# The last four feature tiles of a gated MLP's down projection: plain products or a fourth chunk of block products

## The chip, the cores and the metric

The kernel runs on one core of one Trainium2 chip. The metric is device time of one execution in microseconds (us); the time before is the median of three runs. A profile is one execution taken by the hardware profiler. TensorE is called PE there (PEld is its loading of weights), VectorE DVE, ScalarE ACT, GpSimd POOL; SP's queue issues nearly all the DMAs.

## What is computed

One encoder block on x of shape (1024 positions, 1024 channels), in float32: two parallel convolution modules, then the part that matters here, a gated MLP with 2816 features and a last RMSNorm.

```python
h = rmsnorm(x, norm_ffn_g[l])
g = dwconv(jnp.einsum("bsd,df->bsf", h, w_gate[l]), conv_ffn_w[l])   # 3 taps over positions
v = jnp.einsum("bsd,df->bsf", h, w_up[l])
x = x + jnp.einsum("bsf,fd->bsd", jax.nn.silu(g) * v, w_down[l])
...
return rmsnorm(x, norm_final_g)
```

## The kernel before

Channels lie on the 128 partitions, positions along a row of 1024, split in two halves of 512 (h = 0, 1). The 2816 features are 22 tiles (`f`), the 1024 output channels are 8 blocks (`d`). Every matmul is done with numbers split in a high and a low part: `split` (L130) writes `hi` by a copy on ScalarE and `lo` by a subtraction, in the down stage on VectorE, and a product of 128 x 128 by 128 x 512 is three matmuls.

**Block products.** To save matmuls the kernel treats two feature tiles and two output blocks and the two halves as 2 x 2 blocks and computes seven products where the plain way has eight. On the side of the activations these need seven operands: `B11`, `B21`, `B22` and four differences `T1` to `T4`. For a pair of feature tiles `ff_done` (L607) forms the differences with four subtractions on GpSimd and stores all seven, 256 KB each, in DRAM (`yd`). On the side of the weights `Sums` (L504) forms `S1` to `S4` on GpSimd. `Pair` has one method for each product, `m1` to `m7`, which accumulate in three PSUM banks `a`, `b`, `c` and after each step hand a sum to `Down`'s `after1` to `after7` (L868 on), which add it to the residual block: mostly on VectorE (`add`, L862), after `m1` by a copy on ScalarE and an add on GpSimd (`add_copy`).

**The down stage.** 18 of the 22 tiles go through block products, in three chunks (`NCH`) of three pairs (`PPC`). A chunk is passed over by four objects `Down`, one for each two output blocks, taken as two couples; while one couple multiplies, the weights of the next are loaded and split (`prep1` to `prep3`), and in a chunk's second couple each operand of the next chunk is loaded as soon as its last product is done (`load_op`, L823). The residual blocks `xf` are loaded from `x2d` in DRAM; blocks 3 to 7 (`xd3`, `xr0`, `xr1`) lie where the MLP's temporary tiles `t` lay, and their loads (`load_xd`, L906) are issued when those are released.

**The tail.** The last four tiles (`NTAIL`) go to `ytail` undivided. After the three chunks they are multiplied the plain way: for each half and each output block 4 x 3 matmuls into one bank (`tail_mm`). First all eight blocks of h = 0, then h = 1. `done` (L1026) adds the bank to the residual block on VectorE, squares it on ScalarE, and adds the square to `accs[h]` on VectorE; `scale` (L1022) multiplies the block by the norm's weight on ScalarE. When h = 0 is complete a matmul with ones sums over the channels (`total3`), ScalarE takes the root, VectorE the reciprocal `rf`, and GpSimd scales the eight blocks of h = 0 (`fin`, L1035) beside the products of h = 1. The last block of h = 1 is handled in three pieces (`PIECES`: 192, 192, 128 positions): total, root, reciprocal, scaling of eight blocks (five on VectorE, three on GpSimd) and store.

**What sets the order.** TensorE's order is written out by hand throughout; in the last part, from h = 1 on, those of VectorE, ScalarE and GpSimd too. Before that the other engines' instructions are placed by a scheduler, which puts an instruction where its inputs and buffers allow it. Each engine takes its instructions strictly in order, and SP its DMAs, so that one that waits holds up all behind it.

## Time and profile before

| | us |
|---|---|
| median of 3 runs | 1000.53 (1000.17 to 1000.76) |
| the profiled execution, device time | 1000.93 |
| its span in the trace | 999.1 |
| TensorE busy | 967.5 |
| matmuls of the tail, lines 152 to 154, 192 in all | 25.3 + 24.9 + 24.9 of busy time |
| GpSimd busy | 477.0 |
| DMA | 112.56 MB, 113 GB/s in the mean |

A row of the timeline gives the start in us, the length, the engine, the line, the operation with output and inputs, and in brackets how long the engine had stood idle before and what it waited for. A group row gives busy time and the mean length in ns, then the idle time ahead of it by cause. Matmuls overlap: each shows as 0.39 us, but the next starts 0.23 later.

### The profile page before, as it was taken

Reading aid. Unit: us, or ns where it says so; the run is one execution under the profiler, and the core shown is the slowest. Engines: PE = TensorE matmul, PEld = TensorE weight load, DVE = VectorE, ACT = ScalarE, POOL = GpSimd, SP = SyncE. Lnnn points to the kernel's source line nnn. Section 1 sums busy time; section 2 is a strip of 40 time slices with the busy share of each in tenths; the row PEclk is TensorE's granted clock in tenths of the full one; section 3 lists DMA queues with packets and bytes.
Section 4 is the critical chain, followed back from the end, with each engine's and each line's share of the span. In section 5 each row is a group of like instructions: output and inputs, shape, how many; then the busy total and the mean of one; then the engine's idle time right before and its main releaser. Section 6 shows DMA issues by size and latency. Waiting matters only on the chain.

```text
span 999.1 us, 11602 instructions
## 1 busy us (share of the span) xinstructions
PE 967.5 (97%) x4208; PEld 790.8 (79%) x4208; DVE 755.6 (76%) x888; ACT 452.8 (45%) x632; POOL 477.0 (48%) x303
## 2 busy tenths in 40 slices
PE   7999999999999999999999999999998999999994
PEld 5788888888878887788888888888886787878883
DVE  7899999999578897855655565565569798796556
ACT  7454422234564456434444443444457263544353
POOL 4289754353853006554455456365336744352006
PEclk9999999999999999999999999999999999999998
DMA  6211111113554204143143133134284663643105
GB/s 257 85 44 63 43 45 61 42 64 106 193 190 153 76 0 158 64 148 106 64 145 108 64 124 129 64 101 141 70 287 130 220 207 96 194 127 109 61 1 169
DMA packets 63274, 112.56 MB, mean 113 GB/s; under 512 B 5488, under 2 KB 27120, under 8 KB 62960
## 3 DMA queue, kind: packets, MB, share of 16 engines
q1 hardware_dynamic: 62640, 110.65, 33.1%
q10 hardware_dynamic: 576, 1.17, 0.3%
q8 instruction: 33, 0.54, 0.2%
q14 instruction: 25, 0.20, 0.1%
HBM read 84.79 MB, written 27.00 MB: 112 GB/s over the span
## 4 chain that ended last, share of the span: by engine, by line
PE 81%; DVE 9%; ACT 3%; issue 2%; DMA 1%; POOL 1%; POOLq 0%; SPq 0%; DVEq 0%; ACTq 0%
PE a L557 30%; PE mm L166 20%; PE c L557 15%; PE b L557 7%; DVE r L93 2%; PE c L692 1%; PE a L692 1%; PE mm L153 1%; PE mm L152 1%; PE mm L154 1%; PE y L154 1%; PE y L152 1%; PE y L153 1%; DMA raw<-wgate 1%; ACT whi L131 1%
## 5 line engine op out<-in xcount | busy, mean ns | idle before, releaser
L166 PE MATMUL mm<-r,whi 128*128 128x512 f32 x576 | 155.8, 389 | 0.0
L557 PE MATMUL a<-r,whi 128*128 128x512 f32 x472 | 145.7, 390 | 0.4 <-ACT a L542 0.4
L323 DVE SCALAR_TENSOR_TENSOR cv<-u,cst,cv 128x512 f32<-128x512 f32 x203 | 138.9, 751 | 1.7 <-ACT cv L317 1.2
L511 POOL TENSOR_TENSOR s<-raw,s 128x512 f32<-128x512 f32 (+1 forms) x31 | 57.5, 1854 | 161.5 <-DVE wlo L93 161.5
L166 PEld LDWEIGHTS mm<-r,whi 128*128 128x128 f32 x576 | 108.1, 188 | 22.6
L557 PE MATMUL c<-r,whi 128*128 128x512 f32 x392 | 121.1, 390 | 0.0
L93 POOL TENSOR_TENSOR wlo<-raw,whi 128x1024 fp32r<-128x1024 f32 x30 | 77.5, 2586 | 88.0 <-ACT whi L131 88.0
L131 ACT ACTIVATE whi<-raw 128x1024 fp32r<-128x1024 f32 (+1 forms) x68 | 69.2, 1020 | 103.5 <-PE mm L166 32.0
L557 PEld LDWEIGHTS a<-r,whi 128*128 128x128 f32 x472 | 88.4, 188 | 19.7 <-ACT a L542 0.8
L511 POOL TENSOR_TENSOR s<-up 128x512 f32<-128x512 f32 (+1 forms) x31 | 42.0, 1354 | 116.7 <-DMA up<-wup 96.8
L557 PE MATMUL a<-r,wlo 128*128 128x512 f32 x236 | 92.2, 391 | 2.8 <-DVE wlo L93 2.8
L166 PE MATMUL mm<-r,wlo 128*128 128x512 f32 x288 | 90.0, 389 | 0.0
L557 PEld LDWEIGHTS c<-r,whi 128*128 128x128 f32 x392 | 73.8, 188 | 16.0
L542 ACT ACTIVATE a<-a 128x512 f32<-128x512 f32 x80 | 47.5, 595 | 66.9 <-PE a L557 64.2
L131 ACT ACTIVATE whi<-s 128x1024 fp32r<-128x1024 f32 (+1 forms) x52 | 52.5, 1010 | 53.5 <-PE c L557 39.8
L557 PE MATMUL c<-r,wlo 128*128 128x512 f32 x196 | 76.5, 390 | 0.0
L635 DVE TENSOR_TENSOR t<-a,c 128x512 f32<-128x512 f32 x40 | 27.5, 687 | 64.4 <-ACT a L542 38.1
L557 PE MATMUL a<-r,ahi 128*128 128x512 f32 x224 | 70.5, 396 | 1.4 <-ACT a L542 1.4
L557 PE MATMUL b<-r,whi 128*128 128x512 f32 x232 | 71.4, 389 | 0.0
L93 DVE TENSOR_TENSOR wlo<-s,whi 128x1024 fp32r<-128x1024 f32 (+1 forms) x52 | 64.2, 1236 | 5.8 <-ACT whi L131 5.7
L131 ACT ACTIVATE r<-r 128x512 fp32r<-128x512 f32 x71 | 43.8, 628 | 49.8 <-DMA r<-ydB 23.3
L166 PEld LDWEIGHTS mm<-r,wlo 128*128 128x128 f32 x288 | 54.1, 188 | 11.2
(214 smaller groups left out, 2142.0 us busy)
## 6 DMA issues: line engine op xcount, KB each, us to landing
raw<-wgate SPq DMA_DIRECT2D x22, 512.0 KB, 4.9
up<-wup SPq DMA_DIRECT2D x20, 512.0 KB, 3.6
raw<-win SPq DMA_DIRECT2D x18, 512.0 KB, 3.2
ydT<-t SPq DMA_DIRECT2D x36, 256.0 KB, 3.4
r<-ydT SPq DMA_DIRECT2D x36, 256.0 KB, 3.3
raw<-wout SPq DMA_DIRECT2D x16, 512.0 KB, 3.4
ydB<-t SPq DMA_DIRECT2D x27, 256.0 KB, 5.0
r<-ydB SPq DMA_DIRECT2D x27, 256.0 KB, 4.5
```

Source lines behind the costliest of these rows:

```text
L93: eng.tensor_tensor(out=out, in0=a, in1=b, op=ALU.subtract)
L131: nc.scalar.activation(hi, y, AF.Copy)
L152: nc.tensor.matmul(out, whi, hi, start=first, stop=False)
L153: nc.tensor.matmul(out, whi, lo, start=False, stop=False)
L154: nc.tensor.matmul(out, wlo, hi, start=False, stop=last)
L166: nc.tensor.matmul(outs[h], w, a[h][z], start=s0, stop=s1)
L323: nc.vector.scalar_tensor_tensor(fin if k == KC - 1 else acc, src, w, acc, ALU.mult, ALU.add)
L511: self.eng.tensor_tensor(out=self.t[:, i * self.w : (i + 1) * self.w], in0=a, in1=b, op=op)
L542: nc.scalar.activation(t, b, AF.Copy)
L557: nc.tensor.matmul(out, w[wz][:, k, :], x[xz], start=first and k + wz + xz == 0, stop=k == n - 1 and wz == 1, skip_group_check=not first)
L635: nc.vector.tensor_tensor(out=out, in0=a, in1=b, op=op)
L692: nc.tensor.matmul(out, w[wz][:, k, :], xz, start=first and k == 0 and wz == 0 and xz is hi, stop=not first and k == 3 and wz == 1)
```

## The change

The plain tail is gone. The four last tiles become two more pairs, which `ff_done` treats like the others, and a fourth chunk of two pairs (`NPL`): `fin4`, four objects `Down` (`a4`, `b4`, `c4`, `d4`) with six matmuls for each product. Their order is written out by hand: first the products that complete h = 0 of all eight blocks, `m1`, `m6`, `m2`, `m7`, `m4`, then `m5` and `m3`, which complete h = 1. `final` takes the place of `done`: squares are added on VectorE for h = 0 and for h = 1 on GpSimd (`eng`). The last square of h = 0 is not added but given to `total3` as a second operand. An activation with the root's function (`warm`) is written ahead of the last two products of h = 0. In the first couple, `after5` goes by ScalarE and GpSimd instead of VectorE. In the last scaling VectorE takes all eight blocks of the first two pieces, and GpSimd takes three blocks of the last piece only.

```diff
-NTAIL = NF - 2 * NCH * PPC
+NPL = NF // 2 - NCH * PPC
...
-        if f >= NF - NTAIL:
-            nc.sync.dma_start(ytail[f - (NF - NTAIL)], cc)
-            return
         ys[f] = cc
...
+    def count(ch):
+        return PPC if ch < NCH else NPL
...
+            self.h12, self.h34 = h12, h34 or w34[self.e]
...
         def after5(self):
-            self.add(1, 1, self.c)
+            if self.early:
+                self.add_copy(1, 1, copy_of(self.c, "c5"))
+            else:
+                self.add(1, 1, self.c)
...
+    fin4 = [Down(NCH, dp) for dp in range(2)]
+    fin4 += [Down(NCH, 2 + e, rblocks[28 + 2 * e : 30 + 2 * e], rblocks[32 + 2 * e : 34 + 2 * e]) for e in range(2)]
+    couples.append(fin4[:2])
...
-        for i, pair in enumerate(couples):
+        for i, pair in enumerate(couples[:-1]):
             ch = pair[0].ch
-            reload = i % 2 and ch + 1 < NCH
+            reload = i % 2
...
-    def total3(a):
+    def total3(*a):
         m = bank2("total")
-        nc.tensor.matmul(m, ones, a, start=True, stop=True)
+        for i, x in enumerate(a):
+            nc.tensor.matmul(m, ones, x, start=i == 0, stop=i == len(a) - 1)
         return m
...
-    def done(b, d, h):
+    def final(d, h, eng=nc.vector, first=0, alone=None):
         x = half(xf[d], h)
-        nc.vector.tensor_tensor(out=x, in0=b, in1=x, op=ALU.add)
-        sq = scr("sq") if d else accs[h]
+        sq = scr("sq") if d != first else accs[h]
         nc.scalar.activation(sq, x, AF.Square)
-        if d and (h, d) != (1, KD - 2):
-            nc.vector.tensor_tensor(out=accs[h], in0=accs[h], in1=sq, op=ALU.add)
+        if d not in (first, alone):
+            eng.tensor_tensor(out=accs[h], in0=accs[h], in1=sq, op=ALU.add)
+        scale(d, h)
         return sq
...
+    a4, b4, c4, d4 = fin4
     with tc.manual_schedule(engines={nc.tensor.engine}):
...
+        for p in (c4, d4):
+            p.m7()
+        nc.scalar.activation(warm, eps_r, AF.Sqrt)
+        c4.m4()
+        final(5, 0)
+        d4.m4()
+        s7 = final(7, 0, alone=7)
...
     with tc.manual_schedule(engines={e.engine for e in (nc.tensor, nc.vector, nc.scalar, nc.gpsimd)}):
...
+        a4.m5()
+        b4.m5()
+        m0 = total3(accs[0], s7)
+        std = scr("std")
+        nc.scalar.activation(std, m0, AF.Sqrt, bias=eps_r, scale=1.0 / D)
+        final(1, 1, first=1)
+        final(3, 1, nc.gpsimd, 1)
+        nc.vector.reciprocal(rf[:, :H], std)
+        c4.m5()
+        final(5, 1, nc.gpsimd, 1)
+        d4.m5()
+        final(7, 1, nc.gpsimd, 1)
+        a4.m3()
+        final(0, 1, nc.gpsimd, 1)
+        b4.m3()
+        final(2, 1, nc.gpsimd, 1)
+        for dd in range(KD):
+            fin(dd, 0, 0, H, nc.gpsimd)
+            if dd % 2:
+                store(dd // 2, 0, 0, H)
+        c4.m3()
+        s6 = final(4, 1, first=1, alone=4)
+        d4.mul(d4.c, "S4", "B22", False)
...
-        for (a, b), m in zip(PIECES, ms):
+        for (a, b), m, n in zip(PIECES, ms, (KD, KD, 5)):
...
             for d in range(KD):
-                fin(d, 1, a, b, *((nc.vector, rp) if d < 5 else (nc.gpsimd,)))
+                fin(d, 1, a, b, *((nc.vector, rp) if d < n else (nc.gpsimd,)))
```

What this does to the order of instructions, at three places. First SP's queue at the passage from the MLP into the down stage, before; `ytail` is the store of a finished tile, the lines below load residual blocks 3 to 7:

```order
L616 DMA ytail_1798<-t_5658 128x1024
L616 DMA ytail_1798<-t_5678 128x1024
L907 DMA xd3_5699<-x2d_1790 128x1024
L907 DMA xr0_5700<-x2d_1790 128x1024 x2
L907 DMA xr1_5701<-x2d_1790 128x1024 x2
```

and now, where `t_5668` and `t_5687` are tiles 20 and 21, and `t_5693` and `t_5694` their differences, which GpSimd forms:

```order
L623 DMA ydB11_1791<-t_5668 128x512
L623 DMA ydT1_1795<-t_5693 128x512
L623 DMA ydB21_1793<-t_5687 128x512
L623 DMA ydB22_1797<-t_5687 128x512
L623 DMA ydT2_1792<-t_5693 128x512
L623 DMA ydT3_1794<-t_5694 128x512
L623 DMA ydT4_1796<-t_5694 128x512
L914 DMA xd3_5720<-x2d_1790 128x1024
L914 DMA xr0_5721<-x2d_1790 128x1024 x2
L914 DMA xr1_5722<-x2d_1790 128x1024 x2
```

The loads of x now stand behind seven stores, three of which wait for GpSimd's last subtractions. Second, GpSimd at the same place, now; `s` are sums of weights, `a1` and `c5` copies of PSUM banks that are added to residual blocks:

```order
L90 TENSOR_TENSOR t_5693<-t_5668 128x512
L510 TENSOR_TENSOR s_5799<-up_5796 128x384
L90 TENSOR_TENSOR xd0_5497<-xd0_5497,a1_5861 128x512
L510 TENSOR_TENSOR s_5799<-s_5799,raw_5779 128x384
L90 TENSOR_TENSOR t_5693<-t_5687,t_5693 128x512
L90 TENSOR_TENSOR t_5694<-t_5687,t_5668 128x512
L90 TENSOR_TENSOR t_5694<-t_5687,t_5693 128x512
L90 TENSOR_TENSOR xd0_5497<-xd0_5497,c5_5886 128x512
L510 TENSOR_TENSOR s_5789<-raw_5772,s_5789 128x384
```

Before, the four rows that write `t` and the one that adds `c5` were not there. Third, the end of GpSimd's program: before, the first half's scaling by `rf` followed directly on the last add to a residual block of the three chunks; now five sums of squares (`acc31`) stand ahead of it:

```order
L90 TENSOR_TENSOR xr1_5722<-xr1_5722,a0_7267 128x512
L1002 TENSOR_TENSOR acc31_7089<-acc31_7089,sq_7393 128x512
L1002 TENSOR_TENSOR acc31_7089<-acc31_7089,sq_7406 128x512
L1002 TENSOR_TENSOR acc31_7089<-acc31_7089,sq_7418 128x512
L1002 TENSOR_TENSOR acc31_7089<-acc31_7089,sq_7429 128x512
L1002 TENSOR_TENSOR acc31_7089<-acc31_7089,sq_7440 128x512
L1008 TENSOR_TENSOR xd0_5497<-xd0_5497,rf_7367 128x512 x2
```

Of the early activation with the root's function ScalarE's order shows the following: it stands (L1052) near the start of the program, behind the first two activations of the opening norm's loop (the difference at the end of this section); at the end the load of the table is where it was, directly ahead of the first half's root:

```order
L1000 ACTIVATE sq_7363<-xr1_5722 128x512
L995 ACTIVATE xr1_5722<-xr1_5722,cst_90 128x512
L1063 ACT_TABLE_LOAD
L1063 ACTIVATE std_7389<-total_7386,eps_r_92 128x512
L1000 ACTIVATE acc31_7089<-xd0_5497 128x512
```

and ScalarE's order at the start of the program, as a piece of the difference (`c` is a block of `x`, `acc` and `sq` belong to the first norm):

```order
 L221 ACTIVATE acc_118<-c 128x512
 L224 ACTIVATE sq<-c 128x512
+L1052 ACTIVATE warm<-eps_r 128x1
 L213 ACTIVATE r_94<-c,cst 128x512 x2
 L224 ACTIVATE sq<-c 128x512 x2
```

One row is new there; the load of the table at the end has not moved.

More of the change, by code (lines that the diff above doesn't have):

```diff
@@ new lines, in block_kernel @@
+        for p in (a4, b4):
+            p.m1()
+        for p in couples[-2]:
+            p.m3()
+        load_op(NCH, "B22")
+        for p in (a4, b4):
+            p.prep3()
+        for p in (a4, b4):
+            p.m6()
+        for p in (c4, d4):
+            p.prep1()
+        for p in (a4, b4):
+            p.m2()
+            final(2 * p.dp, 0)
+        for p in (c4, d4):
+            p.prep2()
+            p.prep3()
+        for p in (a4, b4):
+            p.m7()
+        for p in (c4, d4):
+            p.m1()
@@ new lines, in block_kernel @@
+        for p in (a4, b4):
+            p.m4()
+            final(2 * p.dp + 1, 0)
+        for p in (c4, d4):
+            p.m6()
+        for p in (c4, d4):
+            p.m2()
+            final(2 * p.dp, 0)
+        for p in (c4, d4):
+            p.m7()
+        nc.scalar.activation(warm, eps_r, AF.Sqrt)
[3 more added lines that the diff above has]
+        s7 = final(7, 0, alone=7)
+    rf = rup.tile([P, S], F32, tag="up", name="rf")
+    with tc.manual_schedule(engines={e.engine for e in (nc.tensor, nc.vector, nc.scalar, nc.gpsimd)}):
+        a4.m5()
[21 more added lines that the diff above has]
+        d4.mul(d4.c, "S4", "B22", False)
+        last = d4.c
+        x = half(xf[KD - 2], 1)
```

109 lines of the change are left out of this document (26 added, 83 removed).

## The prediction

> **What bounds the kernel now.** I read the page's first block and the windows by stage, then the chain of work that ended last, then the timelines around the places where TensorE stops.
>
> ```profile
> span 999.1 us, 11602 instructions
> ...
> PE 967.5 (97%) x4208; PEld 790.8 (79%) x4208; DVE 755.6 (76%) x888; ACT 452.8 (45%) x632; POOL 477.0 (48%) x303
> ...
> 750.00:800.00 50.00, 45.50 (x189) 36.03 (x189) 42.22 (x43) 24.61 (x38) 35.11 (x22) 0.97 0.57 179
> ...
> 950.00:999.00 49.00, 35.76 (x160) 28.92 (x158) 29.95 (x46) 20.61 (x33) 16.21 (x17) 0.92 0.26 86
> ```
>
> In the window rows the length is followed by the busy times of PE, PEld, DVE, ACT and POOL. TensorE is the limit of the down stage; it loses 4.5 us in 750 to 800 and 13 us at the very end, and little between. So a matmul that is removed is worth its slot only if what stands behind the last matmul gets no longer. The chain says what stands there:
>
> ```profile
> 909.37 4.08 PE c L557 x18
> ...
> 968.91 0.70 DVE xd L1028
> ...
> 986.13 1.28 DVE rp L1092
> 987.43 0.34 ACT rf L1093
> 987.79 1.15 DVE xd L1037 x4
> ```
>
> One matmul is 4.08 / 18 = 0.227 us, and from 968.9 us the chain has left TensorE for adds, squares, reciprocals and the last scaling.
>
> **The matmuls.** The old tail has 16 groups of 4 x 3 matmuls, 192; the fourth chunk has 4 pairs x 7 products x 6, 168. That is 24 x 0.227 = 5.4 us less TensorE time; the second operand in the first half's sum gives back 0.9.
>
> ```profile
> 933.57 0.39 PE L557 MATMUL a<-r,alo 128*128 128x512 f32 x1
> ...
> 965.28 0.86 PE total L1019 x2
> ```
>
> Between chunk three's last A22 product and the last product that the first half needs lie 150 matmuls (chunk three's S4, 18, and 11 steps of 12): 933.8 + 150 x 0.227 = 967.8, in PSUM at **968.0**. Call it T. In the old order the second half's squares begin at 963.3 (below), with seven groups of 12 matmuls, 19 us, still to run; now the first half's statistics start at T, and only 6 products of 6 matmuls (8.2 us) are left to run beside them. This decides the end.
>
> **The end, forward from T.** Durations, from the timeline:
>
> ```profile
> 2.47 0.20 ACT L208 ACTIVATE warm<-eps_r 128x1 f32<-128x1 f32 x1
> ...
> 963.32 0.63 ACT L1030 ACTIVATE acc<-xd 128x512 f32<-128x512 f32 x1 [1.33 <-DVE xd L1028]
> ...
> 963.98 0.72 ACT L1024 ACTIVATE xd<-xd,cst 128x512 f32<-128x512 f32 x1
> ...
> 966.71 0.69 DVE L1032 TENSOR_TENSOR acc<-acc,sq 128x512 f32<-128x512 f32 x1 [0.70 <-ACT sq L1030]
> ...
> 967.45 1.28 ACT L1067 ACT_TABLE_LOAD   x1
> ...
> 968.75 0.69 ACT L1067 ACTIVATE std<-total,eps_r 128x512 f32<-128x512 f32 x1
> ...
> 970.91 3.35 DVE L1069 RECIPROCAL rf<-std 128x512 f32<-128x512 f32 x1
> ...
> 984.43 0.42 ACT L1088 ACTIVATE std<-total,eps_r 128x192 f32<-128x192 f32 x1 [0.25 <-PE total L1085]
> ...
> 992.20 0.95 DVE L1092 RECIPROCAL rp<-std 128x128 f32<-128x128 f32 x1
> ```
>
> Block 5's product is in PSUM at 966.65, added by 967.4 and squared on ScalarE by 968.05; ScalarE scales it, squares block 7 until 969.4, scales it until 970.15, and then loads the root's table until 971.4. The table is not loaded early: the added activation waits for nothing, so the new order has it among ScalarE's first rows, where the same table is already in place (at most 0.20 us, as the first activation of that kind took), and the load ahead of the late root stays. That costs little. VectorE adds block 7 from T on and ends its last sum at 969.5 (2 x 0.69); the two-operand total (2 x 0.86) then ends at 971.2, so the table is late by 0.2 us. The root ends at 972.1, the reciprocal at 975.5. TensorE stands still for 1.5 us at T, which is covered: its last product ends at 979.5, and others end later.
>
> For now ScalarE is the chain: a square and a scale, with gaps 1.38 us, for each block of the second half. Two are done before 975; block 5's add waits behind the reciprocal and ends at 976.1, and then the squares end at 976.7, 978.1, 979.4, 980.8 and 982.2. GpSimd adds five of them, the last from 980.8 on. What such a sum costs there:
>
> ```profile
> L90 POOL TENSOR_TENSOR xd<-xd,a 128x512 f32<-128x512 f32 x10 | 18.9, 1897 | 15.2 <-ACT a L542 15.2
> ...
> L90 POOL TENSOR_TENSOR xr<-xr,a 128x512 f32<-128x512 f32 x6 | 7.7, 1287 | 5.8 <-ACT a L542 5.6 <-DMA xr<-x2d 0.2
> ...
> 977.55 1.66 DVE L1032 TENSOR_TENSOR acc<-acc,sq 128x512 f32<-128x512 f32 x1 [0.70 <-ACT sq L1030]
> ...
> 974.40 5.95 POOL L1037 TENSOR_TENSOR xd<-xd,rf 128x512 f32<-128x512 f32 x4 [63.03 <-DVE rf L1069]
> ...
> 993.54 1.28 POOL L1037 TENSOR_TENSOR xr<-xr,rf 128x128 f32<-128x128 f32 x3 [0.95 <-ACT rf L1093]
> ...
> 995.89 0.90 SPq L1046 DMA_DIRECT2D outT<-xr  x2
> ```
>
> A 128x512 sum on GpSimd takes 1.29 us beside a quiet VectorE and 1.90 beside a busy one, and VectorE's own sum 0.69 or 1.66. I take 1.4: the sum is complete at 982.2. The first piece's total ends 1.2 us later (six passes of 192 columns, 1.0, and the 0.25 before the root), the root at 983.8, the reciprocal at 985.1, the copy at 985.5. Then VectorE scales all eight blocks (8 x 0.29 = 2.3), where it had five: a piece now takes 1.28 + 0.36 + 2.3 = 3.9 us, before 3.0 (from 986.1 to 992.2 for two). Two pieces end at 991.8; the third (0.95, 0.3, five of at most 0.29) by 994.5. GpSimd meanwhile scales the first half, 8 blocks from 982.2, and here I take 1.35, near the quiet row, since VectorE's scaling reads its factor from PSUM: 993.0, then its three short ones (1.28), 994.3. SP's queue holds the first half's last store at 993.0 and six more behind it at 0.45 each, the last issued at 996.2 instead of 996.8. The tail so gains **0.6 us**; with 1.29 throughout 1.0, with 1.49 (5.95 / 4) it loses 0.3, with 1.9 some 4. So 5.4 us of matmuls are nearly all given back.
>
> The Trainium skill's page "SBUF — State Buffer" (section SBUF: two separate sides) says that a VectorE operation with two SBUF inputs and a GpSimd operation that reads SBUF take one port in turns, the loser blocked for a whole instruction. The 0.69 and 1.66 agree. By that rule GpSimd's scaling would run at the quiet 1.29, and the tail gains 1.0.
>
> **The passage into the down stage.** The last four feature tiles now take part in the block products: per pair four GpSimd subtractions, and seven stores of 256 KB for two of 512 KB. All of it stands on SP ahead of loads.
>
> ```profile
> 740.00:750.00 10.00, 10.00 (x45) 8.21 (x44) 4.20 (x6) 3.98 (x9) 2.47 (x2) 1.00 0.91 342
> ...
> 746.40 0.63 ACT L131 ACTIVATE r<-r 128x512 fp32r<-128x512 f32 x1 [6.02 <-DMA r<-ydB]
> ...
> 776.33 3.35 PE L557 MATMUL a<-r,r 128*128 128x512 f32 x7 [2.76 <-DVE r L93]
> ...
> 780.74 2.02 POOL L90 TENSOR_TENSOR xd<-xd,a 128x512 f32<-128x512 f32 x1
> ...
> 781.52 2.32 DVE L614 TENSOR_TENSOR t<-t 128x1024 f32<-128x1024 f32 x1
> ...
> 784.30 0.38 SPq L907 DMA_DIRECT2D xd<-x2d  x1
> ...
> 789.37 0.69 DVE L863 TENSOR_TENSOR xd<-xd,a 128x512 f32<-128x512 f32 x1 [1.91 <-DMA xd<-x2d]
> ...
> 801.30 2.52 DVE L93 TENSOR_TENSOR r<-r 128x512 fp32r<-128x512 f32 x2 [2.29 <-ACT r L131]
> ...
> 804.24 4.24 PE L557 MATMUL a<-r,r 128*128 128x512 f32 x18
> ...
> 834.52 4.35 PE L557 MATMUL a<-r,r 128*128 128x512 f32 x18 [1.41 <-DVE xd L863]
> ```
>
> First pair: before chunk zero's B21 load stand 0.8 MB more; at 342 GB/s (the last column) that is 2.3 us on a load ScalarE already waits 6.0 for. VectorE then works nearly without pause until TensorE's 2.76 us wait at 776; an add moved forward and small pauses take up most of it. **+0.3**, between 0 and 2.3.
>
> Second pair: the product of tile 21 ends at 783.8, and before, the loads of x for blocks 3 to 7 went out at 784.3. Now three subtractions come between (GpSimd is busy until 784.5 with one more ahead, then 3 x 1.5, to 789), and the load of block 3 goes into a buffer that the T2 store must have read (issued at 786, landing about 3.4 later by its row): out at 790, landed, with the 5.1 us of before, at 795 instead of 789.4. VectorE stands at its add of block 3 until then; behind it wait both S4 splits, two adds and the first xr add, which TensorE needs by 804.2: 795 + 6 operations (4.7 us) = 799.7, so 4.5 us remain. The loads of chunk one's B11 go out later too, but VectorE had 2.29 us of waiting there. After that it works without a pause up to the 1.41 us wait at 834.5, which gets some longer: **+0.6**. Ends: -1.4 (two 0.69 us adds leave VectorE for ScalarE and GpSimd, and the wait goes) and +6 (GpSimd at 1.90 per operation, loads landing in 8).
>
> Fourth chunk: its slots from 933.8 on put the first pair's B21 product at 944.7, and only then is a buffer free for the third pair's weights, needed at 948.8. ScalarE (0.63) and VectorE (0.69) split them, each behind one or two splits of sums that GpSimd delivers at about 945; by their rows they are ready at 947.6, 1.2 us early. The sums have 256 columns, which no row shows (192 columns take 0.59 us below, 384 take 1.28); I take 0.8. **+0.3**, between 0 and 2.
>
> ```profile
> ydT<-t SPq DMA_DIRECT2D x36, 256.0 KB, 3.4
> ...
> L511 POOL TENSOR_TENSOR s<-raw,s 128x384 f32<-128x384 f32 x12 | 15.3, 1279 | 47.7 <-DVE wlo L93 47.7
> ...
> L1037 POOL TENSOR_TENSOR xr<-xr,rf 128x192 f32<-128x192 f32 x6 | 3.4, 587 | 3.3 <-ACT rf L1093 3.3
> ```
>
> Sum: -0.6 + 0.3 + 0.6 + 0.3 = +0.6. The profiled execution took 1000.93 us (1.8 around its span), 0.40 over the median of 1000.53, so 1001.5 against the one and **1001.1** against the other.
>
> **Rivals.** (1) *Slower: VectorE behind the x loads.* If block 3 lands after 799.5 the 804.2 product waits, and VectorE, late by as much, makes the wait at 834.5 longer again. GpSimd at 1.90 and a slower store and load give 802.5, 3 us late: 1003.5 to 1006. For it: that queue has two more links than before; against: 4.5 us of room. 25%. (2) *Faster.* The two adds taken off VectorE end the 1.41 us wait, the first pair costs nothing, and the tail gains 1.0: 1000.5 - 2.4, 998.1, less if the 776 wait shrinks. For it: VectorE ends each of these waits; against: GpSimd's new work blocks it. 18%. (3) *Late weights in the fourth chunk* if GpSimd's short sums take 1.3: TensorE waits 3 us, T is 971 and the whole end moves: 1003.5. 7%. (4) *The table costs more than its row.* That the early load doesn't do what it says is in the forecast already; had it worked, it would save 0.2 us. But if a switch held ScalarE for twice the 1.28 of its row, every later square would come 1.3 later: 1002.4. Against it: the root starts 0.02 us after the load. The Trainium skill's page "ScalarE: Activation LUTs" (What ACT_TABLE_LOAD costs) does put a drain of 1380 ns on top of each load; the trace shows none here. 4%. Forecast: 46%.
>
> **How the numbers follow.** This kernel can be told from no change at about 0.2%, 2.0 us: 998.5 to 1002.5. Faster is rival 2 (18%), slower rivals 1 and 3 (32%), the rest the same (50%). The range cuts a tenth at each side: 997.5 from rival 2's better half, 1005.5 from rival 1's worse.
>
> **What would show it.** PE 168 matmuls for 192, and T near 968 plus the waits; the table load still directly ahead of the late root; the last square near T + 14 with VectorE and TensorE waiting; eight GpSimd scalings after it; in 784 to 800 VectorE idle for a DMA 6 us longer. Wrong if GpSimd's sums or x loads are much slower, or VectorE's backlog at 834 vanishes.

## The result, and the profile after

The changed kernel takes **1008.12 us** (median of 4 runs, 1007.47 to 1012.91), the one before on the same chip 1000.35: a ratio of 1.0089 (95% 1.0076 to 1.0101), 7.8 us slower. The forecast, no difference, was wrong, and the time lies outside its range. The profiled execution took 1007.47 us with a span of 1005.3, so 6.2 of the 7.8 us can be followed in the traces; the rest is scatter between executions.

The page's first lines after, and the windows by stage in the columns of before:

```profile
span 1005.3 us, 11721 instructions
PE 965.8 (96%) x4186; PEld 788.1 (78%) x4186; DVE 772.0 (77%) x908; ACT 460.1 (46%) x653; POOL 514.6 (51%) x332
...
800.00:850.00 50.00, 45.20 (x190) 36.28 (x189) 41.82 (x54) 21.80 (x35) 23.28 (x18) 0.97 0.55 173
850.00:900.00 50.00, 50.00 (x221) 41.10 (x220) 41.78 (x54) 24.36 (x39) 25.29 (x19) 1.00 0.58 174
...
950.00:1000.00 50.00, 38.23 (x162) 30.66 (x160) 38.48 (x66) 27.74 (x48) 22.88 (x22) 0.92 0.18 60
```

TensorE is busy 1.7 us less: the 22 matmuls that are gone (24 less, 2 more in the total) are 5.0 us, but others ran longer. From 850 to 950 it doesn't stop. What is new is in 800 to 850: 190 matmuls, where before had 214. TensorE's timeline after shows the two waits there:

```profile
815.05 0.73 PE L556 MATMUL a<-r,ahi 128*128 128x512 f32 x2 [1.78 <-DVE xr L864]
...
839.13 3.27 PE L556 MATMUL a<-r,r 128*128 128x512 f32 x7 [2.98 <-DVE xd L864]
```

The second is the wait that stood at 834.52 with 1.41 us: it ends **4.6 us later**. Behind it come only 7 matmuls in 3.27 us. The windows after, right behind it, say why (the seventh number is the granted clock); the second fence is the same stretch of the run `e14` below, after a wait of 2.97 us:

```profile
839.00:842.00 3.00, 2.87 (x7) 2.32 (x8) 3.00 (x5) 0.47 (x1) 0.25 (x1) 0.50 0.01 3
842.00:845.00 3.00, 3.00 (x15) 2.43 (x14) 1.97 (x4) 0.00 (x0) 0.00 (x0) 0.96 0.00 0
```

```profile
839.00:842.00 3.00, 2.94 (x13) 2.46 (x14) 3.00 (x5) 0.82 (x2) 0.18 (x1) 1.00 0.01 3
```

TensorE ran at half clock for 3 us: it did 7 matmuls where it does 13 at the full clock, so 1.4 us were lost.

To compare kernels I use TensorE's **lag**: how much later than in before's trace the first `b` product of a couple starts.

| couple starts in before at | 765.90 | 800.16 | 828.86 | 859.25 | 887.96 | 917.36 |
|---|---|---|---|---|---|---|
| lag after, us | 0.70 | 0.71 | 3.05 | 6.06 | 6.05 | 5.41 |

So 5.4 us come from the passage into the down stage. The last product that the first half needs is in PSUM at 973.6 (last row 973.20 + 0.40), forecast 968.0: 5.6, so the fourth chunk brought 0.2 more. From there to the end of the span pass 31.7 us, where the forecast amounts to 30.5 (last store issued at 996.2, then the 2.3 of before), so the tail cost 0.6 where it was to gain 0.6. 5.4 + 0.2 + 0.6 = 6.2.

The tail's timeline after, of ScalarE, GpSimd, TensorE and SP:

```profile
975.75 1.28 ACT L1063 ACT_TABLE_LOAD   x1
...
982.47 5.36 POOL L1002 TENSOR_TENSOR acc<-acc,sq 128x512 f32<-128x512 f32 x4 [1.57 <-ACT sq L1000]
987.79 5.12 POOL L1008 TENSOR_TENSOR xd<-xd,rf 128x512 f32<-128x512 f32 x4
...
987.89 0.59 PE L1090 MATMUL total<-acc,ones_r 128*128 128x192 f32 x2 [2.73 <-POOL acc L1002]
...
1001.95 0.93 SPq L1017 DMA_DIRECT2D outT<-xr  x2
```

The sum of squares ends at 987.8, 14.2 us after the last product of the first half, as forecast; GpSimd then scales at 5.12 / 4 = 1.28 us a block.

### The profile page after: what moved, and what is told of

Read it like the earlier page. It is cut to its first block, busy times and chain, and to the rows that moved or that the text cites. A ratio compares the mean times of both kernels' runs of the same rounds, so it can differ in the third digit from the quotient of the medians.

```text
span 1005.3 us, 11721 instructions
## 1 busy us (share of the span) xinstructions
PE 965.8 (96%) x4186; PEld 788.1 (78%) x4186; DVE 772.0 (77%) x908; ACT 460.1 (46%) x653; POOL 514.6 (51%) x332
## 4 chain that ended last, share of the span: by engine, by line
PE 72%; DVE 7%; POOL 5%; issue 5%; DMA 3%; ACT 3%; SPq 0%; POOLq 0%; DVEq 0%; ACTq 0%
PE a L556 27%; PE mm L166 19%; PE c L556 13%; PE b L556 7%; DVE r L93 2%; POOL s L510 2%; PE c L688 1%; PE a L688 1%; PE mm L153 1%; PE mm L152 1%; PE mm L154 1%; DMA r<-ydB 1%; POOL t L90 1%; POOL xd L90 1%; DMA raw<-wgate 1%
## 5 line engine op out<-in xcount | busy, mean ns | idle before, releaser
L556 PE MATMUL a<-r,whi 128*128 128x512 f32 x496 | 153.4, 390 | 1.0 <-ACT a L541 0.9
L510 POOL TENSOR_TENSOR s<-raw,s 128x512 f32<-128x512 f32 (+2 forms) x35 | 60.2, 1719 | 171.9 <-DVE wlo L93 171.3
L131 ACT ACTIVATE whi<-raw 128x1024 fp32r<-128x1024 f32 (+2 forms) x72 | 71.6, 998 | 103.9 <-PE mm L166 32.1
L510 POOL TENSOR_TENSOR s<-up 128x512 f32<-128x512 f32 (+2 forms) x35 | 45.7, 1306 | 116.7 <-DMA up<-wup 96.8
L556 PE MATMUL a<-r,wlo 128*128 128x512 f32 x248 | 97.1, 391 | 3.1 <-DVE wlo L93 3.1
L90 POOL TENSOR_TENSOR t<-t 128x512 f32<-128x512 f32 x44 | 69.0, 1580 | 20.0 <-DVE t L613 20.0
L556 PE MATMUL a<-r,ahi 128*128 128x512 f32 x240 | 75.8, 397 | 3.3 <-DVE xr L864 1.8
L131 ACT ACTIVATE whi<-s 128x1024 fp32r<-128x1024 f32 (+2 forms) x54 | 53.7, 995 | 54.1 <-PE c L556 38.2
L556 PE MATMUL b<-r,whi 128*128 128x512 f32 x248 | 76.4, 389 | 0.0
L93 DVE TENSOR_TENSOR wlo<-s,whi 128x1024 fp32r<-128x1024 f32 (+2 forms) x54 | 67.3, 1246 | 5.9 <-ACT whi L131 5.7
```

Source lines behind the costliest of these rows:

```text
L90: nc.gpsimd.tensor_tensor(out=out, in0=a, in1=b, op=op)
L93: eng.tensor_tensor(out=out, in0=a, in1=b, op=ALU.subtract)
L131: nc.scalar.activation(hi, y, AF.Copy)
L510: self.eng.tensor_tensor(out=self.t[:, i * self.w : (i + 1) * self.w], in0=a, in1=b, op=op)
L556: nc.tensor.matmul(out, w[wz][:, k, :], x[xz], start=first and k + wz + xz == 0, stop=k == n - 1 and wz == 1, skip_group_check=not first)
```

## Experiments

Every run was timed beside before on the same chip (before's medians: 1000.24 to 1000.86 us). The best of those that compute everything, 1004.2, is still slower than before. After a run's expectation stand its median, its ratio to before with the 95% interval, and what its trace shows.

### Which part costs

`e1` leaves the last pair's four subtractions out: its operands are stored straight from the two tiles, so the output differs.

```diff
-        pool(half(t12, 0), half(ye, 1), half(ye, 0), ALU.subtract)
...
+        if f == NF - 1:
+            t12, t34 = ye, yo
+        else:
+            pool(half(t12, 0), half(ye, 1), half(ye, 0), ALU.subtract)
```

> The changed kernel, but the last pair of feature tiles (20 and 21) forms no differences: its T1 to T4 are stored straight from the two tiles (four subtractions on GpSimd left out, the seven stores stay; the output differs). Theory A, the GpSimd chain of four subtractions holds up the loads of x and GpSimd's sums of weights: the load of block 3 goes out by 787 instead of 791.7, VectorE's wait of 4.41 us there falls under 2, TensorE's waits at 815 (1.78) and 839 (2.98) shrink to under 1.5 in all, and the span falls from 1005.3 to 1001 to 1002. Theory B, the bytes or the number of the stores, or the order of SP's queue: the waits stay, span 1004 or more.

1004.40 us, ratio 1.0043 (1.0028 to 1.0057), and the wait is back to 1.71 us (TensorE's timeline of `e1`):

```profile
836.24 4.35 PE L556 MATMUL a<-r,r 128*128 128x512 f32 x18 [1.71 <-DVE xd L869]
```

The lag at 917 is 1.7. Without the last pair's four subtractions the time is 3.7 us less (1008.12 to 1004.40, and the intervals of the two ratios don't meet): that they cause this part of the loss is shown.

`e2`: these four on VectorE.

```diff
+            if f == NF - 1:
+                nc.vector.tensor_tensor(out=out, in0=a, in1=b, op=ALU.subtract)
+            else:
+                pool(out, a, b, ALU.subtract)
```

> The changed kernel, but the last pair's four subtractions run on VectorE. Theory A (GpSimd's chain): 4 x 0.69 = 2.8 us on VectorE in place of 7.8 on GpSimd, the load of block 3 goes out at 787 to 788, and the span falls to 1002 to 1003. Rival, VectorE is the bound of this passage whatever the loads do: its 2.8 us more come back as waits of TensorE at 815 and 839, span 1005 to 1007.

1007.36, 1.0071 (1.0056 to 1.0086); wait until 840.21, 2.81 us. Moving the subtractions to VectorE brings nothing. It is no test of early loads, though: SP's timeline of `e2` has the load of block 3 at

```profile
793.00 0.44 SPq L919 DMA_DIRECT2D xd<-x2d  x1
```

as late as after: now weight loads (`raw`), which wait too, stand ahead of it.

`e3`: `after5` of the first couple on VectorE again.

```diff
-            if self.early:
-                self.add_copy(1, 1, copy_of(self.c, "c5"))
-            else:
-                self.add(1, 1, self.c)
+            self.add(1, 1, self.c)
```

> The changed kernel, but after5 of the first couple adds on VectorE again, as before the change. If the copy and the add on GpSimd (1.59 and 2.00 us, ahead of the sums of weights and of the adds to xr) are part of the loss: GpSimd delivers the sums 1.6 us earlier, span 1004 or less. If the relief of VectorE is worth what the faster rival of the prediction gave it: two adds of 0.69 come back on VectorE, span 1005.7 to 1006.7. If neither sets the waits: 1005.3 within 0.4.

1008.84, 1.0084 (1.0069 to 1.0099): the same time, lost at another place. In the one trace the wait at 839 is not there, and an earlier one is (TensorE's timeline of `e3`):

```profile
801.39 1.19 PE L556 MATMUL c<-r,r 128*128 128x512 f32 x4 [2.55 <-DVE xd L864]
```

VectorE stood there for block 3 until 799.31. TensorE's lag at 800 is 9.1 (after: 0.7), at 917 it is 7.3. So giving `after5` to ScalarE and GpSimd gained no time in the end, but in this trace it decides where the time is lost.

### The differences formed later

A pair stores its four halves only; its differences are formed from DRAM while TensorE is in the down stage, long before the fourth chunk needs them:

```diff
+        if f // 2 in DEFER:
+            for o, t, h in (("B11", ye, 0), ("T1", ye, 1), ("B21", yo, 0), ("B22", yo, 1)):
+                nc.sync.dma_start(yd[o][:, f // 2, :], half(t, h))
+            return
```

`e5` does so for the last pair beside the reload of chunk two's operands, `e6` for both new pairs. `e10` (both pairs) and `e10b` (the last one) do it in the first couples of chunks one and two, where no operand is reloaded; `e16` does it for the first new pair alone. The edit of `e10`:

```diff
+            if i == 2:
+                differences_2(10, *differences_1(10))
+                xy = differences_1(9)
+            if i == 4:
+                differences_2(9, *xy)
```

> The changed kernel, but the last pair stores its two tiles as four halves, and its four differences are formed later, in the chunks, from DRAM (seven more DMAs there), so that nothing of GpSimd stands ahead of the loads of x. Theory A (what costs in the passage is the last pair's GpSimd chain ahead of the loads of x and of the sums of weights): TensorE's waits at 815 and 839 go, its lag behind the kernel before, 5.4 us at the start of chunk three's b product, falls to 0.7 to 1.7, span 1001 to 1002 (as without the differences, 1001.5, plus nothing). Rival (what costs is that GpSimd and the DMA queues have more to do in all): the seven later DMAs and four subtractions cost elsewhere what they save here, span 1003 to 1006.

1009.02, 1.0091 (1.0074 to 1.0108). The passage is nearly as before (wait until 836.43, 1.40 us, lag 1.9), but 60 us on the same thing happens again, and the lag at 917 is 6.2. SP's timeline of `e5`, then TensorE's:

```profile
860.10 0.32 SPq L927 DMA_DIRECT2D ydT<-d  x1
862.07 0.32 SPq L929 DMA_DIRECT2D ydT<-dz  x1
862.44 0.42 SPq L931 DMA_DIRECT2D d<-ydB  x1
862.95 1.35 SPq L824 DMA_DIRECT2D r<-ydT  x3
```

```profile
897.25 5.02 PE L557 MATMUL a<-r,r 128*128 128x512 f32 x14 [2.68 <-DVE xd L870]
```

Stores that wait for GpSimd stand on SP ahead of T2's loads, which before went out at 857.9.

> As e5_late_last, with the differences of the pair before (tiles 18 and 19) formed late too. If the first pair's differences and stores make the lag of 0.7 to 3.3 us that TensorE has at 766 in the runs so far: lag there under 0.4, span 1000 to 1001. If that lag is scatter of the DMA from run to run, or comes from something else: between 0.7 and 2 as before, span 1001 to 1002.5.

1010.64, 1.0101 (1.0085 to 1.0116): the same, a little worse.

> As e6_late_both, but the stores that wait for the late subtractions stand in SP's queue in the first couples of chunks one and two, where no operand of a next chunk is loaded (830 to 848 and 888 to 905). Theory A2 (a store that waits for GpSimd costs by what stands behind it on SP; the subtractions and bytes themselves are nearly free): the passage is as in e6 (lag of TensorE 0.6 at 860) and the waits at 873 and 898 go, lag at most 1 at the b product near 918, span 999.5 to 1001. Rival (the work itself costs, wherever it stands): lag at that product 3 or more, span 1003 or more.

1006.75, 1.0068 (1.0055 to 1.0081); lags 0.05, -1.53, -0.72, 2.29, 4.51, 4.83. The passage now gains, and two waits for `whi`, the high part of the weights, behind it (2.81 us, with half clock, and 1.00) give it back. The weights' loads stand behind the new stores on SP; that this is why they are late was not tested.

> As e10_both_placed for the last pair alone; the pair of tiles 18 and 19 forms its differences in the passage as in the changed kernel. If that first pair costs 0.7 us or more (lag at 766 of 0.7 to 3.3 in the runs that have it, 0.46 in the one without): lag at 766 0.7 to 3.3, span 0.3 to 2.5 above e10_both_placed. If it costs nothing: equal to it within 0.4.

1004.21 (1003.08 to 1009.31), 1.0051 (1.0035 to 1.0068), much as `e1`. Its profiled run is the slowest of the six, with a wait until 839.25 and a lag of 3.0 already at 766, so its trace doesn't stand for the median.

> The changed kernel with the differences of tiles 18 and 19 alone formed late. If this pair makes the lag at 766: under 0.5 there (0.7 to 3.3 in the ten runs with it), median 1006 to 1007. If the lag is given back later: the lag at 922 stays 5 or more, median 1008.

1009.82, 1.0097 (1.0084 to 1.0109). The lag at 766 is gone (-0.18), yet the wait ends at 840.09 after 4.20 us. In this trace the first pair's lag is no term of its own: the wait at 839 swallows it.

### The tail

`e4`: the five sums on VectorE, pieces split five to three again.

```diff
-        final(3, 1, nc.gpsimd, 1)
+        final(3, 1, first=1)
...
-        for (a, b), m, n in zip(PIECES, ms, (KD, KD, 5)):
+        for (a, b), m, n in zip(PIECES, ms, (5, 5, 5)):
```

> The changed kernel, but the second half's squares are added on VectorE and the last scaling is split five to three in all pieces, as before the change. GpSimd is free for the first half's scaling from the reciprocal on (981.1 instead of 987.8). If GpSimd's queue is what makes the end late: pieces of 3.0 instead of 3.9 us, span about 1003.5. If VectorE pays for it (each add now stands behind a sum that waits for its square, 1.95 us for a block, or 2.3 with a sum at 1.66 beside GpSimd's scaling, for five blocks from 981): the last square comes at 991 to 993 instead of 987.4, and the span is 1006 to 1009.

1012.63, 1.0118 (1.0101 to 1.0134), slower than either expectation. TensorE's timeline there, against 2.73 us for GpSimd after:

```profile
997.16 1.01 PE L1090 MATMUL total<-acc,ones_r 128*128 128x192 f32 x2 [6.47 <-DVE acc L1002]
```

`e7`: the second half's squares rounded and summed by matmul.

```diff
+            for t in a:
+                for m, (p, q) in zip(ms, PIECES):
+                    nc.tensor.matmul(m[:, p:q], ones_r, t[:, p:q], start=t is s1, stop=False)
```

> The changed kernel, but all squares of the second half are summed by matmuls with ones, from squares that ScalarE writes as fp32r (rounded), no sums on GpSimd; ScalarE squares before it scales; the last scaling is split five to three in all pieces. Theory C (the end of the changed kernel is set by GpSimd: five sums of 1.29 us hold the first half's scaling until 987.8, which forces VectorE to scale all eight blocks at 3.9 us a piece): GpSimd scales from 981 on, the first piece's root comes at 987.5 instead of 989.2, pieces take 3.0, the tail gains 2.5 to 3.5, span 1002 to 1003. Rival (ScalarE's squares and VectorE's reciprocals set the end whatever GpSimd does, or the scaling on both engines slows VectorE): gain under 1, span 1004.5 or more.

1008.02, 1.0078 (1.0063 to 1.0093): no gain in the time, and 0.6 us in the tail of the trace (31.1). The sums wait 1.61 us for VectorE to empty a PSUM bank, and TensorE's last products end later.

`e8` gives the early activation an input that exists only late, which does move the table's load:

```diff
+        nc.scalar.activation(warm, s6[:, :1], AF.Sqrt)
...
-        nc.scalar.activation(warm, eps_r, AF.Sqrt)
```

> The changed kernel, but the activation meant to load the root's table reads the square of block 6, so that it stands late in ScalarE's order, in its idle time before block 5. The prediction says that a load done early saves 0.2 us: the first half's root starts 0.2 us sooner after the total, and the end comes 0 to 0.3 us sooner relative to TensorE's last product of the first half (973.6 to 1005.3, 31.7 us, becomes 31.4 to 31.7). Rival: ScalarE is the chain there, and the whole 1.28 us goes: 30.4.

One execution, 1010.88; ScalarE's timeline:

```profile
973.86 1.28 ACT L1050 ACT_TABLE_LOAD   x1
...
980.56 0.69 ACT L1063 ACTIVATE std<-total,eps_r 128x512 f32<-128x512 f32 x1 [1.26 <-PE total L990]
```

The root then waits for the total as long as the load took; from the last first-half product to the end pass 31.8 us, after 31.7. So an early load of the table gains nothing here.

`e11` makes the first half's reciprocal in four pieces of 128, with VectorE's adds between, and squares block 2 ahead of a scaling:

```diff
-        nc.vector.reciprocal(rf[:, :H], std)
+        def rec(i):
+            nc.vector.reciprocal(rf[:, i * P : i * P + P], std[:, i * P : i * P + P])
+        rec(0)
...
+        rec(1)
```

> The changed kernel, but the first half's reciprocal is taken in four pieces of 128, each between two adds of the second half, and the last square stands ahead of a scaling. Theory D (the end waits for ScalarE's squares because VectorE stands in the one reciprocal of 3.35 us while four products are ready): the squares of blocks 5, 7, 0, 2, 4 come 1 to 2 us sooner after the last product of the first half, the first piece's total too, end 1.7 to 2.4 us sooner by the tail (after that product 29.3 to 30 us instead of 31.7). Rival (four pieces at 0.95 cost 3.8 instead of 3.35 and VectorE's adds come no sooner, or GpSimd's sums at 1.29 set the end): gain under 0.7.

1006.81, 1.0065 (1.0053 to 1.0077); the tail lasts 30.7 us, 1.0 less, not the 1.7 to 2.4 expected. The first piece's total is 1.5 us earlier, of which a third is lost by the end.

> e10_both_placed and e11_reciprocal_in_pieces together. If both theories hold the gains add: span 997 to 999, faster than the kernel before by 0 to 2 us.

`e12` (`e10` and `e11`): 1004.19, 1.0043 (1.0031 to 1.0055), its profiled span 1001.9, not 997 to 999. With it the rest above before is waits in the down stage: its lag at 917 is 2.9, and its span is 2.8 above before's.

### The link between the subtractions and the wait

`e13` loads block 3 into a buffer that is free early, by ScalarE's queue, so that VectorE needn't stand at it; `e14` adds the tail of `e11`, and `e15` late differences for the first pair too.

```diff
-        for d in range(3, KD):
+        nc.scalar.dma_start(xf[3], x2d[3])
+        for d in range(4, KD):
             load_xd(d)
```

> The changed kernel, but residual block 3 lies in a buffer that is free early, and its load is issued by ScalarE's queue, ahead of the stores of the differences instead of behind them; GpSimd's subtractions stay where they were. Link 1 (VectorE stands at block 3's add until its load lands, so the splits and the loads behind them on SP are late): VectorE's wait of 4.41 us at 796 falls under 1, the loads of chunk one's T2 go out by 802 instead of 805.2, TensorE's waits at 815 and 839 shrink, its gain of lag from 766 to 922 falls from 4.7 to 1 to 2.5, median 1004 to 1006. Link 2 (GpSimd's sums of weights, 7 us late at 792.7, release the buffers of the next weights late): VectorE's wait goes but the T2 loads stay at 804 to 805 and the lag gained stays above 3.5, median 1007 or more.

1008.59, 1.0081 (1.0068 to 1.0094). VectorE's wait for block 3 is gone and the big wait is not (until 839.71, 3.39 us): VectorE's standing at block 3 is not the link. What came is what was expected of link 2 (T2's loads at 804.19, 5.5 us of lag gained after 766), so GpSimd's late sums of weights stay a candidate. `e2` and `e17` speak against it without settling it: in `e2` these sums end 2.1 us sooner than after (794.5 for 796.6), in `e17` the weights no longer stand ahead of T2, and the wait ends at 840.21 and 838.84.

> e13_block3_early with the reciprocal in pieces of e11: the two places do not touch, so 1.0 us less than e13 (e11 against the changed kernel: 31.7 to 30.7 us after the last product of the first half).

> e14_block3_and_tail with the differences of tiles 18 and 19 formed late, their stores in the first couple of chunk one. If that pair costs its 1 to 2 us at 766 and the repairs add: median 1000 to 1003, lag at 766 under 0.5. If a lead at 766 is given back at the wait near 835 (which ended at 834.5 to 835.2 in the kernel before, e6, e10 and e12, whatever the lead): no less than e14.

1006.24, 1.0056 (1.0044 to 1.0068) and 1007.06, 1.0067 (1.0054 to 1.0080); the wait ends at 839.06 and 839.89. In `e14` that is the tail's 1.0 and no half clock behind the wait (its row above); the wait itself ends where it did.

`e17` writes SP's order by hand, B11, T2 and B21 ahead of the weights:

```diff
 L914 DMA xr_5722<-x2d 128x1024 x2
-L830 DMA raw<-wdown 128x3x128
-L818 DMA r_96<-ydB_1791 128x512
-L830 DMA raw<-wdown 128x3x128
-L818 DMA r_96<-ydB_1791 128x512 x2
-L830 DMA raw<-wdown 128x3x128 x2
+L818 DMA r_96<-ydB_1791 128x512 x3
+L818 DMA r_97<-ydT_1792 128x512 x3
...
```

> After's kernel with one thing changed: in chunk zero's second couple SP's order is written out, so that the loads of chunk one's B11, T2 and B21 stand ahead of the third pair's weights (raw, up), which wait for GpSimd's sums and for the loads of x to land. Nothing is left out; the last pair's subtractions stay where they are. Theory (SP's queue: the operand loads are late because the weight loads ahead of them wait): the first T2 load goes out between 798 and 801 us instead of 805.2, the wait of 0.7 us at 815 is gone, the wait that ends at 839.1 (2.98 us) ends at 835 to 837 without the half clock behind it, the lag of TensorE against before is under 2.5 us at 922, and the median is 1003.0 to 1005.5. Rival A (the backlog on VectorE and ScalarE themselves is the link, not the loads): T2 goes out early, but the wait still ends at 838.5 to 840.5, and the median is 1007 to 1010. Rival B (the weights are now the late ones, since their loads stand behind nine operand loads): the wait at 839 is smaller, but the lag at 831.9 grows beyond 3 us with a wait for whi or wlo ahead of it, and the median is 1006 to 1011.

1008.55, 1.0079 (1.0066 to 1.0093). T2 goes out at 799.03, 6 us sooner than after, and the wait ends where it did, as rival A expected. VectorE's timeline of `e17`, then TensorE's:

```profile
798.19 0.69 DVE L864 TENSOR_TENSOR xd<-xd,a 128x512 f32<-128x512 f32 x1 [5.43 <-DMA xd<-x2d]
...
804.77 0.69 DVE L93 TENSOR_TENSOR r<-r 128x512 fp32r<-128x512 f32 x1 [2.46 <-ACT r L131]
...
838.02 0.67 DVE L864 TENSOR_TENSOR xd<-xd,a 128x512 f32<-128x512 f32 x1
```

```profile
838.84 3.75 PE L556 MATMUL a<-r,r 128*128 128x512 f32 x8 [3.68 <-DVE xd L864]
```

From its first B11 split at 804.77 on VectorE works without a pause to the add that ends the wait, 33.2 us from start to start. Before it began that split at 801.30 and needed 32.4. So in these two traces the end of the wait is set by when B11 has landed, with some 33 us of VectorE's work behind, and `e17` made T2 early but B11 late: ScalarE could split it at 804.11, after at 802.47.

`e18` takes four adds (2.7 us) off VectorE in that stretch, in `add_a`:

```diff
-            if self.early:
+            if self.ch == 0:
                 self.add_copy(m, h, copy_of(self.a, "a1"))
```

> After's kernel with one condition changed: in chunk zero's second couple the sums after m6 and m7 (four adds of 0.68 us that VectorE makes into xr between 800 and 817 us) are copied by ScalarE and added by GpSimd, as those of the first couple are. Nothing else moves: SP's order stays, the last pair's subtractions stay. Theory (VectorE's own work is the bound: from its product of tile 21 to its add that ends the wait at 839 it needs 55.8 us, in before 52.2, and the four adds stand in this stretch; the wait of 1.78 us at 815 is for one of them): that wait is gone or under 0.8 us, the wait that ends at 839.1 ends between 835.5 and 837.5 with under 2.2 us and without the half clock, TensorE's lag at 922 is 1.5 to 3.5 us instead of 5.4, the median 1003.8 to 1005.8. Rival A (the operand loads bind: T2 still goes out at 805 and B22 at 832): the adds only make room for standing, VectorE waits 2 us or more for loads between 803 and 838, the wait still ends at 838.5 or later, median 1007 to 1010. Rival B (GpSimd's four more adds of 1.3 to 1.9 us hold up its sums of weights and collide with VectorE, whose operations of 0.68 us get longer): a new wait for wlo or s between 815 and 835, median 1007 or more.

1009.29, 1.0084 (1.0070 to 1.0098): a miss, and not a clean test. The scheduler put a weights' load on SP ahead of T4's, against the run's premise that SP's order stays; SP's waits in 806 to 834, ScalarE's and TensorE's timelines:

```profile
SPq L830 <- POOL s L510: 12.0, 2, 11.7
```

```profile
830.65 1.33 ACT L131 ACTIVATE r<-r 128x512 fp32r<-128x512 f32 x2 [9.47 <-DMA r<-ydT]
```

```profile
832.52 1.22 PE L556 MATMUL a<-r,whi 128*128 128x512 f32 x2 [5.60 <-ACT a L541]
```

The wait at 815 went (0.28), that at 839 too, and one of 5.60 took their place: SP stood 11.7 us at a weights' load, T4 came late, ScalarE's copies stood behind its split.

## Why the prediction was wrong

**The step that failed** is the second pair's "+0.6" in the passage: it is 4.6 up to the wait at 839, and 1.4 of half clock on top (0.6 is given back later, 0.4 of it because before's wait at 893 is not there after). Its first half held. Block 3 landed at 796.0 (forecast 795), and the product at 804.2, which had 4.5 us in hand, doesn't wait at all (804.95, no wait). What failed is the sentence after: "The loads of chunk one's B11 go out later too, but VectorE had 2.29 us of waiting there", and that the wait at 834.5 "gets some longer". B11's loads went out no later, the first at 795.21 (before: 795.59), but they landed later. ScalarE splits them first; its timeline before, then after:

```profile
800.63 1.95 ACT L131 ACTIVATE r<-r 128x512 fp32r<-128x512 f32 x3 [3.65 <-DMA r<-ydB]
```

```profile
802.47 0.63 ACT L131 ACTIVATE r<-r 128x512 fp32r<-128x512 f32 x1 [4.80 <-DMA r<-ydB]
```

SP's timeline after:

```profile
791.70 0.32 SPq L914 DMA_DIRECT2D xd<-x2d  x1
792.19 1.81 SPq L914 DMA_DIRECT2D xr<-x2d  x4
...
801.20 3.88 SPq L830 DMA_DIRECT2D up<-wdown  x4
805.17 1.46 SPq L818 DMA_DIRECT2D r<-ydT  x3
```

The x loads go out 7.4 us later than before's 784.30, and five of 512 KB are 2.6 MB. I counted who waits for them, and not what their transfer does to those behind. The windows of before, then of after, `e1` and `e17` (the last two numbers: DMA share, GB/s):

```profile
784.00:792.00 8.00, 8.00 (x37) 6.50 (x35) 4.92 (x8) 2.22 (x4) 6.62 (x6) 1.00 0.92 323
792.00:804.00 12.00, 12.00 (x54) 9.95 (x53) 7.26 (x9) 4.63 (x7) 6.75 (x6) 1.00 1.03 312
...
804.00:810.00 6.00, 6.00 (x28) 4.97 (x27) 6.00 (x10) 4.71 (x9) 0.00 (x0) 1.00 0.72 225
```

```profile
784.00:792.00 8.00, 8.00 (x36) 6.53 (x35) 7.51 (x6) 2.87 (x5) 8.00 (x5) 1.00 0.35 131
792.00:804.00 12.00, 12.00 (x54) 9.95 (x53) 5.96 (x7) 2.92 (x4) 11.09 (x9) 1.00 1.01 362
804.00:816.00 12.00, 10.22 (x45) 8.14 (x45) 9.36 (x12) 7.99 (x14) 4.70 (x4) 1.00 1.05 335
```

```profile
784.00:792.00 8.00, 8.00 (x36) 6.53 (x35) 6.81 (x7) 3.17 (x6) 6.65 (x6) 1.00 0.74 246
```

```profile
784.00:792.00 8.00, 8.00 (x36) 6.54 (x35) 7.90 (x6) 2.75 (x5) 8.00 (x5) 1.00 0.31 116
```

While SP waits for GpSimd's subtractions the DMA engines are two thirds idle for 8 us, and then full until 816, where before they had slack from 804 on. From 784 to 804 there passed 1.05 + 4.34 = 5.39 MB after (8 us at the first rate, 12 at the second) and 6.33 before. The 0.94 MB behind are 2.6 us at 362 GB/s, less than the 4.6 to be explained.

To set all runs side by side, each one's 20 us begin at 784 plus its own lag at 766 (-0.9 to 3.3 us), and that lag is taken off the end of the wait:

| MB moved in the 20 us | runs | the wait ends, less the lag, at |
|---|---|---|
| 6.3 to 6.9 | before, `e1`, `e5`, `e6`, `e10`, `e10b`, `e12` | 834.5 to 836.2 |
| 5.5 to 5.9 | after, `e2`, `e4`, `e7`, `e8`, `e11`, `e13` to `e17` | 837.0 to 840.3 |

`e3` and `e18` moved 5.5 too, and lost their time at 801 and at 832. The upper row is the runs without the last pair's subtractions in the passage, and within a row the MB don't order the ends. So the table goes with what `e1` and `e5` show, and is no separate proof that the lost transfer time is the way. After, `e4`, `e7`, `e8` and `e11` have the same program up to there and end at 838.4 to 839.8; `e13`, `e14` and `e17` at 837.0 to 837.8, so a help of about 1 us from their edits isn't excluded.

The stretch is full, and what `e17` gives T2 it takes from B11; 0.5 MB by another queue (`e13`) leave the rest late. The first B11 load goes out at 795.2 to 795.6 in before, after and `e17`, and ScalarE has it at 800.63, 802.47 and 804.11: the later the x loads ahead of it had gone out (784.30, 791.70, 792.85), the later it came. VectorE shows it in its standing at the operands. The timeline after:

```profile
803.13 0.69 DVE L93 TENSOR_TENSOR r<-r 128x512 fp32r<-128x512 f32 x1 [1.84 <-ACT r L131]
...
805.24 0.69 DVE L93 TENSOR_TENSOR r<-r 128x512 fp32r<-128x512 f32 x1 [1.42 <-ACT r L131]
...
810.60 1.51 DVE L93 TENSOR_TENSOR r<-r,r 128x512 fp32r<-128x512 f32 x1 [1.40 <-ACT r L131]
...
835.93 1.05 DVE L93 TENSOR_TENSOR r<-r 128x512 fp32r<-128x512 f32 x1 [0.36 <-ACT r L131]
837.35 1.04 DVE L93 TENSOR_TENSOR r<-r,r 128x512 fp32r<-128x512 f32 x1 [0.36 <-ACT r L131]
838.31 0.67 DVE L864 TENSOR_TENSOR xd<-xd,a 128x512 f32<-128x512 f32 x1
```

So the 4.6 us divide: VectorE's first B11 split starts 1.8 us later than before (803.13 for 801.30), from there it stands 3.5 us for operands (1.42, 1.40 and twice 0.36) where before it doesn't stand at all, and it works 0.8 us less up to the add, which starts at 838.31 for 833.70. That the subtractions cause the loss is shown (`e1`, `e5`). That the way leads through the lost transfer time is a reading that fits these rows; no run moved the x loads alone ahead of the stores, since their buffers are those the stores read, and GpSimd's late sums stay a candidate beside it, so it is short of shown.

**The half clock** was not priced, though a row of the prediction has it: behind before's wait of 2.76 us at 776, 7 matmuls take 3.35 us, where in `e10` they take 1.88 behind the same wait. It comes and goes between traces (last section): its 1.4 us are in after's trace, not in those of `e2`, `e11` and `e14`.

**The other steps.** *First pair, +0.3*: the lag of 0.7 is real and vanishes into the wait (`e16`). *Fourth chunk, +0.3*: 0.2; the weights came in time. *T and the chain behind it*: relative to T, root, reciprocal and the sum of squares came to within 0.1 us, the squares up to 0.4 sooner. *The table*: cost nothing, as said, and would have brought nothing (`e8`); ScalarE shows no drain after the load. *GpSimd's scaling*: taken as 1.35, measured 1.28 and 1.23. The quiet price held, as by the port rule of the Trainium skill's page "SBUF — State Buffer" (section SBUF: two separate sides), since VectorE's scaling has one of its inputs in PSUM. *The stores*: mis-sized by 1.1. The last five take 3.1 us (999.74 to 1002.88), 0.63 each and not 0.45: -0.6 became +0.6.

**The rivals.** Rival 1 was the nearest, slower by a late load at this place, with 1003.5 to 1006 too low; its mechanism is not the one after (no wait at 804, and `e13` removes VectorE's standing without effect), though `e3`'s trace has it, with block 3 added at 799.31 and the wait at 801.39. It had been priced by GpSimd's and the loads' own durations, without half clock and without the full DMA. Rivals 2, 3 and 4 did not happen.

## What to carry to other kernels

A load that is held up on an in-order queue can cost more than the wait of its reader. Here the transfer engines were two thirds idle meanwhile and full for the 24 us behind, and loads that were issued on time landed late. So count bytes per stretch, and ask if it is full afterwards. Work that was cheap beside a busy TensorE, such as four subtractions, was dear at a passage where buffers change hands, because stores wait for it and loads wait for the stores. And where a stretch has one engine without pauses ahead of a wait (here 32 us of VectorE), a delay at its start comes out at its end.

## What the hardware showed that was not expected

TensorE's half clock. Before a block of 18 matmuls, waits of 1.41 to 1.71 us left it at 4.33 to 4.36 us; after waits of 2.68 to 4.35 us it took 4.34 to 4.36 (`e2`, `e11` and `e14`, waits of 2.81, 2.98 and 2.97), 5.8 to 6.0, or 6.9 to 7.2 us (`e15`, a wait of 4.35). The same wait of 2.98 us cost 1.4 in the changed kernel and nothing in `e11`. The wait near 777 shows the chance best: it lasts 2.73 to 2.76 us in nineteen of the twenty traces, before's among them, and in the 3 us behind it the granted clock is 1.00 in five (`e7`, `e10`, `e12`, `e17`, `e18`) and 0.50 to 0.74 in fourteen. The Trainium skill's page "TensorE: Matmul & The Clock Gate" (Part 1: The HAM clock gate) has the clock halved after an idle window of about 3.4 us that runs freely; the chance character agrees, while here waits from 2.7 us on are enough. It may be part of why the changed kernel, `e10b`, `e11` and `e13` scatter by 4.4 to 6.2 us between runs, where the other edits scatter by 0.7 to 4.0 and before by 1.2 to 3.5. The slowest run of the changed kernel, 1012.91, has the lowest mean granted clock of its four, 0.982 for 0.989 to 0.990, but the slowest of `e11` has the highest of its six, so that is not shown.
